# Seven block products in place of eight for q, k and r of a gated linear attention layer, in two phases with DRAM between them

## The chip, the cores and the metric

The kernel runs on one core of a Trainium2 chip, as one program with one launch. The metric is the device time of one execution in microseconds (us), from the first to the last instruction with what lies around them. The engines are TensorE (PE, matrix products into PSUM banks), VectorE (DVE), ScalarE (ACT), GpSimd (POOL) and SyncE (SP, which here issues nearly all DMA transfers). Each engine takes its own instructions strictly in the order in which the program has them, and waits on semaphores for what others make.

## The reference, cut to what matters

Two layers over a sequence of 1024 tokens with 1024 features, in float32: layer 0 has a mixer of a convolution module and an mLSTM, layer 1 has gated linear attention (GLA), and each layer ends in a SwiGLU FFN. The change touches layer 1's mixer:

```
def gla_mixer(h, w_in, gate_w2, gate_b, head_g, w_out):
    z = h @ w_in
    q, k, v, r, gl = jnp.split(z, [...], -1)
    log_alpha = log_sigmoid(gl @ gate_w2 + gate_b) / GLA_TAU
    o = gla_chunkwise(heads(q), heads(k), heads(v), heads(log_alpha))
    o = head_rmsnorm(o, head_g) * silu(r)
    return o @ w_out
```

There are 4 heads, each with 128 columns of q and of k and 256 of v and of r. h is the RMS-normed input of the layer. The result is added to the layer's input.

## The kernel before, in words

Activations are kept transposed: 8 tiles (k = 0 to 7) of 128 features by 512 tokens, for each of two halves of the tokens. A float32 product is made of three matmuls of a reduced type (`mm3`): every operand is cut into a high part (hH, wH; an ACT copy) and a low part (hL, wL; a DVE subtraction), `split` for activations and `weights` for a weight unit of 128 x 1024, which it loads (tile raw, 512 KB) and cuts (L163 on ACT, L164 on DVE). The matmuls of `mm3` are lines L170 (low weight), L171 (low activation) and L172 (both high). wH and wL have three buffers each, raw has two.

A projection `proj` of 128 columns for one half of the tokens is 8 k's times three matmuls, 24 matmuls of 128x512 into one PSUM bank "mm". The second mixer (`mixer1` with levels off) goes through the list ORDER1: p = v, q and k of a head; r = its r; x = the head's attention (decays, scores, state updates; banks "sm"), o = its norm, the transposes and the product with silu(r), whose result is y, two tiles a head and half, in SBUF; k0 = the cuts of y that the output projection needs. Where a letter a or b follows, only the first or second half of the tokens is meant. q and k leave their banks by an ACT copy (L827). silu(r) is made from a Tanh on ACT (L838) and one DVE operation (L839). x of head 3's second half and o of heads 2 and 3 stand behind k0 and are mixed with the first half of the output projection (`out_proj`, its run for half 0).

The order of each engine's instructions is fixed when the program is built, by a scheduler with a model of durations; `tc.high_priority(offset=...)` puts an instruction ahead of its place, which is how loads and weight cuts come early. SP's queue is one list: a transfer that waits for a buffer holds up all behind it. In layer 0 and in both FFNs the kernel already uses block products with sums of blocks and with DRAM in between.

There is a second branch in the program, the mixer with levels, run when a comparison (`fits`) says that the decays are too strong for the plain form.

Of the kernel before, what the change touches and what calls it, by code (L numbers as in the profile page):

```python
# [67 lines left out]
BOUND = -320.0  # L68

# [6 lines left out]
def trunk_kernel(ctx, tc, xT, cols, gate_b0, ev_vo0, ev_u, ev_cw, ev_out, od_v0, od_u, od_out, gate_w2, fin_row,  # L76
                 w13, w2, out, xsp, rowd, ud, zd, ad, x1, md):
# [627 lines left out]
    def mixer1(h, cut, then, levels):  # L705
        y = [[None, None] for _ in range(KT)]
        with tc.tile_pool(name="m1", bufs=1, reuse_waits="tile") as mp:
            unit = iter(range(30))
            masks = []
            if levels:  # L710
                for w in LEVELS:

                    nb = P // (2 * w)
                    m = mp.tile([P, nb, 2 * w], F32, tag="junk", name=f"mf{w}", bufs=1)
                    POOL.memset(m, 1.0)
                    for half, at in ((m[:, :, w:], 0), (m[:, :, :w], w)):

                        POOL.affine_select(out=half, in_=half, compare_op=ALU.is_ge, fill=0.0, base=-at,
                                           pattern=[[-2 * w, nb], [0, w]], channel_multiplier=1)
                        POOL.affine_select(out=half, in_=half, compare_op=ALU.is_ge, fill=0.0, base=at + w - 1,  # L720
                                           pattern=[[2 * w, nb], [0, w]], channel_multiplier=-1)
                    mu = mp.tile([P, P], U8, tag=f"mk{w}", name=f"mk{w}")
                    DVE.tensor_copy(mu, m.rearrange("p b x -> p (b x)"))
                    masks.append(mu)
                m = mp.tile([P, P], F32, tag="junk", name="mft", bufs=1)
                POOL.memset(m, 1.0)
                POOL.affine_select(out=m, in_=m, compare_op=ALU.is_ge, fill=0.0, base=-1, pattern=[[1, P]], channel_multiplier=-1)
                above = mp.tile([P, P], U8, tag="above", name="above")
                DVE.tensor_copy(above, m)
            else:  # L730
                m = mp.tile([P, P], F32, tag="junk", name="mft", bufs=1)
                POOL.memset(m, 1.0)
                POOL.affine_select(out=m, in_=m, compare_op=ALU.is_ge, fill=0.0, base=0, pattern=[[1, P]], channel_multiplier=-1)
                causal = mp.tile([P, P], U8, tag="causal", name="causal")
                DVE.tensor_copy(causal, m)
                whole = [mp.tile([P, HALF], F32, tag=f"A{i}", name=f"A{i}") for i in range(AB)]
                for t in whole:
                    POOL.memset(t, 0.0)
                least = mp.tile([P, HEADS, 2, 4], F32, tag="least", name="least")
# [37 lines left out]
            def decays(glc):  # L777

                es = []
                for half in range(2):  # L780
# [3 lines left out]
                    glr = mp.tile([P, HALF], F32R, tag="qt", name="glr", bufs=1 if levels else 2)  # L784
# [16 lines left out]
                for half in range(2):  # L801
                    for hd in range(HEADS):
# [6 lines left out]
                        if not levels:  # L809
                            DVE.tensor_copy(least[:, hd, half], lf.rearrange("p (c t) -> p c t", c=4)[:, :, P - 1])  # L810
                if not levels:
                    bounded()

            def bounded():

                m = mp.tile([P, 1], F32, tag="least1", name="least1")
                DVE.tensor_reduce(out=m, in_=least.rearrange("p a b c -> p (a b c)"), axis=mybir.AxisListType.X, op=ALU.min)
                b = bank("sm")
                PE.transpose(b[:1, :P], m, ident)
                n = mp.tile([1, 1], F32, tag="least2", name="least2")  # L820
                DVE.tensor_reduce(out=n, in_=b[:1, :P], axis=mybir.AxisListType.X, op=ALU.min)
                DVE.tensor_scalar(out=fits, in0=n, scalar1=BOUND, scalar2=None, op0=ALU.is_ge)

# [17 lines left out]
            def at_once(hd, half, q, k):  # L841

                A = whole[(2 * hd + half) % AB]
                pb = bank("sm")
                for c in range(4):
                    cs = slice(c * P, (c + 1) * P)
                    PE.matmul(pb[:, cs], k[:, cs], q[:, cs], start=True, stop=True)  # L847
                DVE.copy_predicated(A.rearrange("p (c t) -> p c t", c=4), causal.unsqueeze(1).to_broadcast([P, 4, P]),
                                    pb.rearrange("p (c t) -> p c t", c=4))
                return A  # L850

            def by_levels(bs, q, k):
# [43 lines left out]
                return A  # L896

            def head_mix(hd, half, q, k, v, st):
                bs = bsum[hd][half]
                b3 = bs.rearrange("p (c t) -> p c t", c=4)  # L900

                qt = mp.tile([P, HALF], F32, tag="qt", name=nm("qt"), bufs=1 if levels else 2)
                ACT.activation(qt, bs, AF.Exp, scale=1.0 / 16)
                ea = mp.tile([P, 4], F32, tag="ea", name=nm("ea"), bufs=2)
                ACT.activation(ea, b3[:, :, P - 1], AF.Exp, scale=1.0 / 16)
                DVE.tensor_tensor(out=qt, in0=qt, in1=q, op=ALU.mult)

                n = 4 - half
# [699 lines left out]
```

## Time and profile before

| What | Value |
|---|---|
| Time, median of 3 runs | 2133.81 us (2132.85 to 2134.03) |
| The profiled execution's own time, its span | 2133.76 us, 2132.0 us |
| Mean granted TensorE clock | 0.998 |
| Moved by DMA in the span | 279.04 MB, mean 131 GB/s |
| Second mixer's first matmul | at 1074.55 us |

The profile is of one execution. A line names the engine, the line of the program (L170), the tiles written and read without their numbers, the shape, and how long it was busy. PEld is the loading of weights into TensorE, which overlaps the matmuls. Matmuls are pipelined, so their busy times overlap; the distance of two starts is what one costs. "<- DVE wL L164" behind a wait names what ended it. A stretch of the span is given by its start and end in us; the share of busy time there belongs to that stretch alone. A letter q after an engine (SPq) is its queue of issues.

### The profile page before, as it was taken

The page shows a single profiled execution, that of the slowest core. Times are in us where ns is not written, and L with a number is a line of the kernel's source. Part 1 is how long each engine was busy: PE and PEld are TensorE (multiplying, and loading weights), DVE is VectorE, ACT ScalarE, POOL GpSimd, SP SyncE. Part 2 cuts the span into 40 slices and gives each one's busy share as a digit, 9 for nine tenths or more (in the row PEclk, how much of TensorE's full clock was granted, in tenths as well). Part 3 has the DMA queues.
Part 4 walks back from the last instruction along what each step waited for, and adds up shares of the span by engine and source line. Part 5 has one row for each costly group of instructions (what it writes and reads, how often), then busy time and mean ns, then how long its engine had stood idle before and what let it go on. Part 6 is the DMA issues. An engine that isn't in the chain of part 4 may idle for free.

```text
span 2132.0 us, 27718 instructions
## 1 busy us (share of the span) xinstructions
PE 2117.0 (99%) x10511; PEld 1795.9 (84%) x10511; DVE 1437.3 (67%) x2190; ACT 835.6 (39%) x1368; POOL 2.9 (0%) x15
## 2 busy tenths in 40 slices
PE   9999999999999999999999999999999999999998
PEld 8889988888888888888888989888888888888887
DVE  7555788777776666877875323367877666677686
ACT  6302327553222222444664434344522222235453
POOL 0000000000000000000000000000000000000000
PEclk9999999999999999999999999999999999999999
DMA  4233453654443334734421111154544333374344
GB/s 160 90 115 116 146 139 109 212 175 172 162 144 109 109 108 160 250 115 149 129 73 40 40 50 30 44 194 168 201 146 166 119 104 109 102 273 142 96 124 145
DMA packets 138222, 279.04 MB, mean 131 GB/s; under 512 B 22304, under 2 KB 35488, under 8 KB 138080
## 3 DMA queue, kind: packets, MB, share of 16 engines
q1 hardware_dynamic: 137808, 276.92, 39.6%
q8 instruction: 85, 1.39, 0.3%
q14 instruction: 57, 0.47, 0.1%
q10 hardware_dynamic: 272, 0.26, 0.0%
HBM read 210.51 MB, written 66.62 MB: 130 GB/s over the span
## 4 chain that ended last, share of the span: by engine, by line
PE 97%; DVE 1%; ACT 1%; DMA 1%; issue 0%; SPq 0%; DVEq 0%; ACTq 0%
PE mm L170 21%; PE mm L171 21%; PE mm L172 21%; PE sm L172 10%; PE sm L170 10%; PE sm L171 10%; PE sm L407 2%; PE sm L937 1%; PE sm L936 1%; PE sm L939 1%; DMA wb<-rowd 0%; PE sm L847 0%; PE sm L966 0%; PE sm L620 0%; PE sm L587 0%; PE sm L622 0%
## 5 line engine op out<-in xcount | busy, mean ns | idle before, releaser
L171 PE MATMUL mm<-hL,wH 128*128 128x512 f32 x1420 | 554.5, 391 | 0.2 <-DVE hL L335 0.2
L172 PE MATMUL mm<-hH,wH 128*128 128x512 f32 x1420 | 553.7, 390 | 0.0
L170 PE MATMUL mm<-hH,wL 128*128 128x512 f32 x1420 | 518.0, 391 | 2.1 <-DVE wL L164 1.2
L170 PEld LDWEIGHTS mm<-hH,wL 128*128 128x128 f32 x1420 | 266.5, 188 | 58.8 <-ACT hH L334 1.8
L171 PEld LDWEIGHTS mm<-hL,wH 128*128 128x128 f32 x1420 | 266.7, 188 | 55.9 <-DVE hL L335 1.0
L172 PEld LDWEIGHTS mm<-hH,wH 128*128 128x128 f32 x1420 | 266.7, 188 | 55.5 <-issue 0.2
L171 PE MATMUL sm<-hL,wH 128*128 128x512 f32 x616 | 240.1, 390 | 0.0
L172 PE MATMUL sm<-hH,wH 128*128 128x512 f32 x616 | 239.7, 389 | 0.0
L170 PE MATMUL sm<-hH,wL 128*128 128x512 f32 x616 | 209.0, 390 | 0.0
L143 ACT ACTIVATE wH<-S 128x1024 fp32r<-128x1024 f32 x88 | 93.3, 1060 | 214.1 <-PE sm L172 214.1
L143 ACT ACTIVATE wH<-q 128x512 fp32r<-128x512 f32 x143 | 90.4, 632 | 177.8 <-PE mm L172 100.6
L164 DVE TENSOR_TENSOR wL<-raw,wH 128x1024 fp32r<-128x1024 f32 (+2 forms) x77 | 94.2, 1223 | 82.6 <-ACT wH L163 82.4
L143 DVE TENSOR_TENSOR wL<-q,wH 128x512 fp32r<-128x512 f32 x143 | 98.6, 690 | 73.3 <-ACT wH L143 72.8
L170 PE MATMUL mm<-wH,hL 128*128 128x256 f32 (+2 forms) x512 | 146.4, 289 | 0.6 <-DVE xy L1320 0.6
L171 PE MATMUL mm<-wL,hH 128*128 128x256 f32 (+2 forms) x512 | 146.6, 287 | 0.0
L172 PE MATMUL mm<-wH,hH 128*128 128x256 f32 (+2 forms) x512 | 146.4, 287 | 0.0
L163 ACT ACTIVATE wH<-raw 128x1024 fp32r<-128x1024 f32 (+2 forms) x77 | 81.6, 1060 | 147.1 <-PE mm L172 115.2
L171 PEld LDWEIGHTS sm<-hL,wH 128*128 128x128 f32 x616 | 115.6, 188 | 24.7 <-issue 0.7
L170 PEld LDWEIGHTS sm<-hH,wL 128*128 128x128 f32 x616 | 115.6, 188 | 24.4 <-PE mm L172 0.5
L172 PEld LDWEIGHTS sm<-hH,wH 128*128 128x128 f32 x616 | 115.6, 188 | 24.3 <-issue 0.2
L143 DVE TENSOR_TENSOR wL<-S,wH 128x1024 fp32r<-128x1024 f32 x88 | 107.5, 1221 | 23.9 <-ACT wH L143 23.9
L1124 DVE TENSOR_TENSOR c<-sm,c 128x512 f32<-128x512 f32 x110 | 75.6, 687 | 70.5 <-PE sm L172 70.4
(324 smaller groups left out, 3434.6 us busy)
## 6 DMA issues: line engine op xcount, KB each, us to landing
raw<-in_w SPq DMA_DIRECT2D x108, 512.0 KB
mdT<-c SPq DMA_DIRECT2D x88, 256.0 KB
m<-mdT SPq DMA_DIRECT2D x88, 256.0 KB
mdB<-c SPq DMA_DIRECT2D x66, 256.0 KB
q<-in_w SPq DMA_DIRECT2D x60, 256.0 KB
m<-mdB SPq DMA_DIRECT2D x55, 256.0 KB
raw<-in_od_u SPq DMA_DIRECT2D x22, 512.0 KB
raw<-in_ev_u SPq DMA_DIRECT2D x20, 512.0 KB
```

Source lines behind the costliest of these rows:

```text
L143: ins = ACT.activation(dst[0], src, AF.Copy), lo.tensor_tensor(out=dst[1], in0=src, in1=dst[0], op=ALU.subtract)
L163: first = ACT.activation(hi, raw, AF.Copy)
L164: cuts = lo.tensor_tensor(out=low, in0=raw, in1=hi, op=ALU.subtract)
L170: return (PE.matmul(o, lt[1], rt[0], start=start and not on, stop=False, skip_group_check=on), PE.matmul(o, lt[0], rt[1], start=False, sto ...
L171: PE.matmul(o, lt[0], rt[1], start=False, stop=False, skip_group_check=on),
L172: PE.matmul(o, lt[0], rt[0], start=False, stop=stop, skip_group_check=on))
L407: PE.matmul(o, w[:, m * P:(m + 1) * P], raw[:, e, m:m + NT], start=m == 0, stop=m == SH)
L936: PE.matmul(db[:, cc, :], kw[:, cs], v[:, c, :], start=True, stop=True)
L937: PE.matmul(ob[:, cc, :], A[:, cs], v[:, c, :], start=True, stop=st is None)
L939: PE.matmul(ob[:, cc, :], qt[:, cs], st, start=False, stop=True)
L1124: DVE.tensor_tensor(out=out, in0=a, in1=b, op=ALU.add)
```

## The change

q and k of a head (or its two r tiles) are taken together as a product of 2 by 2 blocks: the weights are split by output column (two of 128) and by input feature (k = 0 to 3 and 4 to 7), the activations by input feature and by half of the tokens. The four results are c11, c12 (first column block, halves 0 and 1), c21 and c22. Eight block products of 12 matmuls become seven, with sums of weight blocks (tile S and in place in raw), sums of activation blocks (T1 to T4) and sums of results.

Phase one (list FIRST) makes the first column block's two products for half 0, A11 B11 and then A12 B21 in the same bank, and copies both states of the bank to DRAM (cd). It also makes v for all heads (those of heads 2 and 3 go to DRAM, vd) and the decays (to DRAM, bd). `transforms` makes T1 to T4 by 16 subtractions of unsplit activations; T1, T3 and T4 go to DRAM (td), T2 is cut at once; `operands` loads the three again and cuts them into the tiles that held h. Phase two (list REST) has for each pair the loads of both weight units, four sums of 512 columns, the cuts of two and a half units, the loads of the two phase-one results into the tiles of c12 and c11, and the products T2, T1, T3, T4 and B22, each a bank of its own but B22, which goes on top of T1's bank once that has been added; six sums read the banks. There are 8 pairs.

Silu is now one ACT function. y of heads 0 and 1 goes to DRAM (yd) and `get` loads it for the output projection: for half 0 into a tile of tag "q", for half 1 two at a time into a raw tile. The normed activations of the mixer's input are kept unsplit beside their parts. Before, the decays' Exp and Ln were made for both halves together, now for each half. The mixer with levels in the other branch stays as it was, and loses the code of the plain form.

```diff
+FIRST = 'q01 q23 v0 v1 v2 t v3 r01 r23'.split()
+REST = 'q0 q1 x0 r0 o0 q2 x1 f0 r1 o1 q3 x2 x3a r2 o2a r3 o3a k0 o2b x3b o3b'.split()
...
-    def mixer1(h, cut, then, levels):
+    def mixer1(h, cut, then):
...
+    def mixer1_at_once(h, b, cut, then):
...
+                        if hd < 2:
+                            ACT.activation(v[half][:, c, :], b[:, :256], AF.Copy)
+                        else:
+                            if c % 2 == 0:
+                                t = tmp()
+                            ACT.activation(t[:, c % 2 * 256:c % 2 * 256 + 256], b[:, :256], AF.Copy)
+                            if c % 2:
+                                SP.dma_start(vd[hd - 2, half][:, c // 2 * HALF:c // 2 * HALF + HALF], t)
...
+                        SP.dma_start(bd[hd, half], lf)
...
+            def first(kind, hds):
+                def aside(hd, i, b):
+                    with tc.high_priority(offset=WOFF):
+                        t = mp.tile([P, HALF], F32, tag="q", name=nm("c"), bufs=QB1)
+                        ACT.activation(t, b, AF.Copy)
+                        SP.dma_start(cd[spot(kind, hd), i], t)
+                ws, bs = [], []
+                for hd in hds:
+                    w, b = weights(od_u[at[kind, hd, 0]], 1024, DVE), bank("mm")
+                    for k in range(4):
+                        mm3(b, wcol(w, k, P), h[0][k], k == 0, k == 3)
+                    aside(hd, 0, b)
+                    ws.append(w)
+                    bs.append(b)
+                for hd, w, b in zip(hds, ws, bs):
+                    for k in range(4, KT):
+                        mm3(b, wcol(w, k, P), h[0][k], False, k == KT - 1, True)
+                    aside(hd, 1, b)
+            hv = {}
+            odd = [True]
+            def transforms():
+                for k in range(4):
+                    b11, b21, b12, b22 = b[0][k], b[0][k + 4], b[1][k], b[1][k + 4]
+                    for i, (o, x, z) in enumerate(((b11, b12, b11), (b12, b22, b12), (b22, b22, b11), (b21, b21, b22))):
+                        behind(DVE.tensor_tensor(out=o, in0=x, in1=z, op=ALU.subtract), made[1])
+                        if i != 2:
+                            SP.dma_start(td[min(i, 2), k], o)
+                    hv["T2", k] = tuple(hp.tile([P, HALF], F32R, tag=f"xy{k + 4 * i}_0", name=nm("T2")) for i in range(2))
+                    split(hv["T2", k], b22, DVE)
+                    hv["B22", k] = h[1][k + 4]
+            def operands():
+                for name, i, o, half in (("T1", 0, 0, 1), ("T3", 1, 0, 0), ("T4", 2, 4, 0)):
+                    for k in range(4):
+                        t = mp.tile([P, HALF], F32, tag="k", name=nm("t"), bufs=QB1)
+                        with tc.high_priority(offset=WOFF):
+                            SP.dma_start(t, td[i, k])
+                        hv[name, k] = hl(o + k, half)
+                        split(hv[name, k], t, DVE)
+            def cutw(x):
+                w = tuple(wp.tile([P, 1088], F32R, tag=t, name=nm(t))[:, :x.shape[1]] for t in ("wH", "wL"))
+                split(w, x, DVE)
+                return w
+            def pair(kind, hd, c11, c12, c21, c22):
+                with tc.high_priority(offset=WOFF):
+                    if odd[0]:
+                        r1, r2 = (mp.tile([P, 1024], F32, tag="raw", name=nm("raw"), bufs=2) for _ in range(2))
+                    else:
+                        r1, r2 = (wp.tile([P, 1088], F32, tag="raw", name=nm("raw"), bufs=2)[:, :1024] for _ in range(2))
+                    odd[0] = not odd[0]
+                    for i, t in ((1, r2), (0, r1)):
+                        SP.dma_start(t, od_u[at[kind, hd, i]])
+                    s = mp.tile([P, 1024], F32, tag="S", name=nm("S"), bufs=1)
+                    lo, hi = slice(0, HALF), slice(HALF, 1024)
+                    DVE.tensor_tensor(out=s[:, lo], in0=r2[:, lo], in1=r2[:, hi], op=ALU.add)
+                    DVE.tensor_tensor(out=s[:, hi], in0=s[:, lo], in1=r1[:, lo], op=ALU.subtract)
+                    w12 = cutw(s)
+                    DVE.tensor_tensor(out=r2[:, lo], in0=r1[:, lo], in1=r2[:, lo], op=ALU.subtract)
+                    w34 = cutw(r2)
+                    DVE.tensor_tensor(out=r1[:, hi], in0=r1[:, hi], in1=s[:, hi], op=ALU.subtract)
+                    w5 = cutw(r1[:, hi])
+                    SP.dma_start(c12, cd[spot(kind, hd), 0])
+                    SP.dma_start(c11, cd[spot(kind, hd), 1])
+                def prod(name, w, o, on=None):
+                    b = on if on is not None else bank("mm")
+                    for k in range(4):
+                        mm3(b, tuple(t[:, o + k * P:o + k * P + P] for t in w), hv[name, k], k == 0, k == 3, on is not None)
+                    return b
+                def add(o, b, x):
+                    DVE.tensor_tensor(out=o, in0=b, in1=x, op=ALU.add)
+                add(c12, prod("T2", w12, HALF), c12)
+                t = prod("T1", w12, 0)
+                add(c22, prod("T3", w34, 0), c12)
+                add(c21, prod("T4", w34, HALF), c22)
+                add(c22, t, c22)
+                add(c12, prod("B22", w5, 0, t), c12)
...
+                bs = mp.tile([P, HALF], F32, tag="bs", name=nm("bs"), bufs=4)
+                with tc.high_priority(offset=WOFF):
+                    SP.dma_start(bs, bd[hd, half])
...
+                    t = y[2 * hd + i][half]
+                    DVE.scalar_tensor_tensor(out=t, in0=b, scalar=c1(C_HG1 + 2 * hd + i), in1=t, op0=ALU.mult, op1=ALU.mult)
+                    if hd < 2:
+                        SP.dma_start(yd[2 * hd + i, half], t)
+            def get(k, half, d, _=None):
+                t = y[k][half]
+                if k < 4:
+                    if half == 0:
+                        t = mp.tile([P, HALF], F32, tag="q", name=nm("y"), bufs=QB1)
+                    else:
+                        if k % 2 == 0:
+                            ld[:] = [mp.tile([P, 1024], F32, tag="raw", name=nm("y"), bufs=2)]
+                        t = ld[0][:, k % 2 * HALF:k % 2 * HALF + HALF]
+                    with tc.high_priority(offset=1000):
+                        SP.dma_start(t, yd[k, half])
+                split(d, t, DVE)
...
+                if what[0] == "q":
+                    q, k = ([mp.tile([P, HALF], F32, tag=t, name=nm("qk"), bufs=QB1) for _ in range(2)] for t in "qk")
+                    pair("q", hd, *q, *k)
+                    heads[hd] = q, k
+                elif what[0] == "r":
+                    for i in range(2):
+                        for half in range(2):
+                            y[2 * hd + i][half] = hp.tile([P, HALF], F32, tag=f"xy{4 * (hd % 2) + 2 * i + half}_1", name=nm("y"))
+                    pair("r", hd, *y[2 * hd], *y[2 * hd + 1])
+                    for i in range(2):
+                        for t in y[2 * hd + i]:
+                            ACT.activation(t, t, AF.Silu)
...
+            r = rstd_half(xs)
+            d, work = [], []
+            for k in range(KT):
+                a = DVE.scalar_tensor_tensor(out=xs[k], in0=xs[k], scalar=c1(g + k), in1=r, op0=ALU.mult, op1=ALU.mult)
+                d.append(hl(k, half))
+                work += [[a], [split(d[k], xs[k], DVE)]]
...
+    layer(1, lambda cut, then: mixer1_at_once(h1, b1, cut, then), od_out, x1, C_FFN + 8, finish)
```

Three places show what moves. The line numbers of `mm3` are L172 to L174 in the new program; the numbers behind a tile's name only tell one tile from another, and they differ between the two programs.

The first place is on TensorE, in phase two, where the product B22 of the first pair stands: bank mm_10857 holds T1 of the pair of head 0's q and k, mm_10966 is the T3 of head 1's pair. In the new order:

```order
L172 MATMUL mm_10966<-hH_1907_10782,wL_10929 128x512
L173 MATMUL mm_10966<-hL_1908_10783,wH_10928 128x512
L174 MATMUL mm_10966<-hH_1907_10782,wH_10928 128x512
L172 MATMUL mm_10966<-hH_1910_10788,wL_10929 128x512
L172 MATMUL mm_10857<-hH_1729_9316,wL_10838 128x512
L173 MATMUL mm_10857<-hL_1730_9317,wH_10837 128x512
```

The twelve matmuls of B22 stand behind the T2, the T1 and ten matmuls of the T3 of the next pair; the two last matmuls of that T3 follow them.

The second place is SP's queue ahead of the first output projection: y tiles from yd, raw is a weight unit of the output projection, xy a tile of the layer's input. In the new order, where before there were only the raw and xy rows of these:

```order
L162 DMA raw_12277<-in_od_out 128x1024
L1247 DMA y_12117<-yd 128x512
L162 DMA raw_12311<-in_od_out 128x1024
L1247 DMA y_12123<-yd 128x512
L1247 DMA y_12129<-yd 128x512
L162 DMA raw_12345<-in_od_out 128x1024
L1247 DMA y_12135<-yd 128x512
L162 DMA raw_12379<-in_od_out 128x1024
L272 DMA xy_2355_12647<-x 128x512
```

The loads of y stand between the weight units, and the four tiles y follow one another through one buffer.

The third place is the start of that projection on TensorE: banks mm_11991 (before) and mm_12251, mm_12285, mm_12319 (now), with hH and hL the parts of y. Before:

```order
L170 MATMUL mm_11991<-hH_2118_11867,wL_11986 128x512
L171 MATMUL mm_11991<-hL_2119_11868,wH_11985 128x512
L172 MATMUL mm_11991<-hH_2118_11867,wH_11985 128x512
L170 MATMUL mm_11991<-hH_2120_11871,wL_11986 128x512
L171 MATMUL mm_11991<-hL_2121_11872,wH_11985 128x512
L172 MATMUL mm_11991<-hH_2120_11871,wH_11985 128x512
L170 MATMUL mm_11991<-hH_2122_11875,wL_11986 128x512
```

and now:

```order
L172 MATMUL mm_12251<-hH_2226_12127,wL_12246 128x512
L173 MATMUL mm_12251<-hL_2227_12128,wH_12245 128x512
L174 MATMUL mm_12251<-hH_2226_12127,wH_12245 128x512
L172 MATMUL mm_12285<-hH_2226_12127,wL_12280 128x512
L173 MATMUL mm_12285<-hL_2227_12128,wH_12279 128x512
L1203 MATMUL sm_11852<-v_11824,kw_11843 128x256
L174 MATMUL mm_12285<-hH_2226_12127,wH_12279 128x512
L172 MATMUL mm_12319<-hH_2220_12115,wL_12314 128x512
L173 MATMUL mm_12319<-hL_2221_12116,wH_12313 128x512
L172 MATMUL mm_12251<-hH_2229_12133,wL_12246 128x512
L172 MATMUL mm_12285<-hH_2229_12133,wL_12280 128x512
```

Before, the first bank takes tile after tile of y without a break; now three banks take each tile as it comes, with a state update (L1203) of head 3 between them.

On ACT the cuts of the same four tiles stood in one row (hH from xy, with two more behind):

```order
L143 ACTIVATE hH_2118_11867<-xy_1811_9880 128x512
L143 ACTIVATE hH_2120_11871<-xy_1820_9944 128x512
L143 ACTIVATE hH_2122_11875<-xy_1971_10944 128x512
L143 ACTIVATE hH_2124_11879<-xy_1980_11008 128x512
L143 ACTIVATE hH_2126_11883<-xy_2082_11612 128x512
L143 ACTIVATE hH_2128_11887<-xy_2091_11676 128x512
```

and now they stand among table loads, squares and Silus:

```order
L145 ACTIVATE hH_2220_12115<-y_12117 128x512
L1218 ACTIVATE junk_11764,ss_9357<-og_11732 128x256
L1224 ACT_TABLE_LOAD
L1224 ACTIVATE ss_9357<-ss_9357,epsc 128x4
L145 ACTIVATE hH_2223_12121<-y_12123 128x512
L165 ACTIVATE wH_12279<-raw_12277 128x1024
L1283 ACT_TABLE_LOAD
L1283 ACTIVATE y_12002<-y_12002 128x512
L1214 ACTIVATE og_11792<-sm_11794 128x512
L1283 ACTIVATE y_12003<-y_12003 128x512
L1218 ACTIVATE junk_11806,ss_9357<-og_11792 128x256
L145 ACTIVATE hH_2226_12127<-y_12129 128x512
```

What follows each cut on ACT now waits for the next load of y or for TensorE.

More of the change, by code (lines that the diff above doesn't have):

```diff
@@ L709, in mixer1 @@
             masks = []
[L710 to L725, printed above, removed]
-                POOL.memset(m, 1.0)
[L727 to L739, printed above, removed]
@@ new lines, in mixer1 @@
+            for w in LEVELS:
+                nb = P // (2 * w)
+                m = mp.tile([P, nb, 2 * w], F32, tag="junk", name=f"mf{w}", bufs=1)
+                POOL.memset(m, 1.0)
+                for half, at in ((m[:, :, w:], 0), (m[:, :, :w], w)):
+                    POOL.affine_select(out=half, in_=half, compare_op=ALU.is_ge, fill=0.0, base=-at,
+                                       pattern=[[-2 * w, nb], [0, w]], channel_multiplier=1)
+                    POOL.affine_select(out=half, in_=half, compare_op=ALU.is_ge, fill=0.0, base=at + w - 1,
+                                       pattern=[[2 * w, nb], [0, w]], channel_multiplier=-1)
+                mu = mp.tile([P, P], U8, tag=f"mk{w}", name=f"mk{w}")
+                DVE.tensor_copy(mu, m.rearrange("p b x -> p (b x)"))
+                masks.append(mu)
@@ L741, in mixer1 @@
+            m = mp.tile([P, P], F32, tag="junk", name="mft", bufs=1)
+            POOL.memset(m, 1.0)
+            POOL.affine_select(out=m, in_=m, compare_op=ALU.is_ge, fill=0.0, base=-1, pattern=[[1, P]], channel_multiplier=-1)
+            above = mp.tile([P, P], U8, tag="above", name="above")
+            DVE.tensor_copy(above, m)
             raw = tmp()
@@ L839, in head_r, with head_mix @@
                         DVE.scalar_tensor_tensor(out=t, in0=e, scalar=1.0, in1=b, op0=ALU.add, op1=ALU.mult)
[L841 to L852, printed above, removed]
+            def head_mix(hd, half, q, k, v, st):
+                bs = bsum[hd][half]
+                b3 = bs.rearrange("p (c t) -> p c t", c=4)
+                qt = mp.tile([P, HALF], F32, tag="qt", name=nm("qt"), bufs=1)
+                ACT.activation(qt, bs, AF.Exp, scale=1.0 / 16)
+                ea = mp.tile([P, 4], F32, tag="ea", name=nm("ea"), bufs=2)
+                ACT.activation(ea, b3[:, :, P - 1], AF.Exp, scale=1.0 / 16)
+                DVE.tensor_tensor(out=qt, in0=qt, in1=q, op=ALU.mult)
+                n = 4 - half
+                kt = tmp()[:, :n * P]
+                kt3 = kt.rearrange("p (c t) -> p c t", c=n)
+                DVE.tensor_tensor(out=kt3, in0=b3[:, :n, P - 1:P].to_broadcast([P, n, P]), in1=b3[:, :n], op=ALU.subtract)
+                ACT.activation(kt, kt, AF.Exp, scale=1.0 / 16)
+                DVE.tensor_tensor(out=kt, in0=kt, in1=k[:, :n * P], op=ALU.mult)
+                kb = bank("sm")[:, :n * P]
+                for c in range(n):
+                    PE.transpose(kb[:, c * P:(c + 1) * P], kt[:, c * P:(c + 1) * P], ident)
+                kw = mp.tile([P, HALF], F32, tag="kw", name=nm("kw"), bufs=1)[:, :n * P]
+                ACT.activation(kw, kb, AF.Copy)
                 A = mp.tile([P, HALF], F32, tag="A", name=nm("A"), bufs=AB)
@@ L1479, in trunk_kernel @@
             h.append(norm_half(xs, C_MIX + 8, half)[0])
-        layer(1, lambda cut, then: mixer1(h, cut, then, True), od_out, x1, C_FFN + 8, finish)
+        layer(1, lambda cut, then: mixer1(h, cut, then), od_out, x1, C_FFN + 8, finish)
 def _layout(i):
```

254 lines of the change are left out of this document (204 added, 50 removed).

## The prediction

> **What bounds the kernel now.** I read the page first (busy shares, then the chain that ended last), then what TensorE (PE) waits for, then the stretch of the second mixer. Page, part 1 and the first row of part 4:
>
> ```profile
> PE 2117.0 (99%) x10511; PEld 1795.9 (84%) x10511; DVE 1437.3 (67%) x2190; ACT 835.6 (39%) x1368; POOL 2.9 (0%) x15
> ...
> PE 97%; DVE 1%; ACT 1%; DMA 1%; issue 0%; SPq 0%; DVEq 0%; ACTq 0%
> ```
>
> PE is busy for 2117.0 of 2132.0 us and 97% of the chain runs through it. What PE waits for in the whole span (in total, times, longest):
>
> ```profile
> PE sm L105 <- DVE t L102: 1.5, 1, 1.5
> PE mm L170 <- DVE wL L164: 1.2, 2, 0.6
> PE mm L170 <- ACT hH L334: 0.9, 1, 0.9
> PE mm L170 <- DVE xy L1320: 0.6, 1, 0.6
> PE sm L622 <- DVE st L628: 0.4, 2, 0.2
> PE mm L171 <- DVE hL L335: 0.2, 1, 0.2
> ```
>
> These add to 4.8 us, and only the 0.6 us on L1320 is at the second mixer's door. So matmuls taken away are time taken away, as long as the others keep up. How far they are from the edge is read by stretches (us; busy PE, PEld, DVE, ACT, POOL; granted clock; DMA share; GB/s): the second mixer up to the first half of its output projection, then a piece of layer 0's FFN and one of layer 1's:
>
> ```profile
> 1074.00:1440.00 366.00, 365.45 (x2060) 322.42 (x2061) 163.24 (x266) 162.31 (x291) 0.00 (x0) 1.00 0.21 69
> ...
> 852.80:906.10 53.30, 53.30 (x237) 44.14 (x236) 45.60 (x74) 23.05 (x41) 0.00 (x0) 1.00 0.73 250
> ...
> 1865.50:1918.80 53.30, 53.30 (x237) 44.14 (x236) 37.91 (x55) 16.85 (x25) 0.00 (x0) 1.00 0.77 274
> ```
>
> In the mixer PE leaves out 0.55 of 366 us, VectorE (DVE) works 45%, ScalarE (ACT) 44%, and DMA moves 69 GB/s. In the FFN pieces PE loses nothing while DVE is at 86% and DMA at 250 to 274 GB/s. That is the yardstick for a mixer that is to be fuller.
>
> **What the change removes from PE.** The price of a 128x512 matmul is its pitch in a steady run, not its busy time:
>
> ```profile
> 1241.10 0.39 PE L172 MATMUL mm<-hH,wH 128*128 128x512 f32 x1
> ...
> 1250.16 0.39 PE L170 MATMUL mm<-hH,wL 128*128 128x512 f32 x1
> ```
>
> Forty matmuls lie between these starts: 9.06 / 40 = 0.2265 us. A pair (q and k of a head, or the two r columns) had four halves of 24 matmuls, 96. Now it has 24 in phase one and five products of 12 in phase two, 84. Eight pairs lose 96 matmuls: 96 x 0.2265 = 21.7 us. The head's matmuls and transposes stay in number.
>
> **What it adds beside PE.** Prices from the groups of the stretch from 1070 to 1440, by form (count, busy, mean ns):
>
> ```profile
> L164 DVE TENSOR_TENSOR wL<-raw,wH 128x1024 fp32r<-128x1024 f32 x31 | 37.8, 1221 | 63.0 <-ACT wH L163 62.9
> L163 ACT ACTIVATE wH<-raw 128x1024 fp32r<-128x1024 f32 x31 | 32.8, 1059 | 74.2 <-PE mm L172 73.7 <-ACT kw L925 0.5
> ...
> L839 DVE SCALAR_TENSOR_TENSOR xy<-t,mm 128x512 f32<-128x512 f32 x16 | 10.9, 681 | 10.7 <-ACT t L838 10.7
> L957 ACT ACT_TABLE_LOAD x8 | 10.3, 1283 | 0.1
> L143 DVE TENSOR_TENSOR hL<-xy,hH 128x512 fp32r<-128x512 f32 x16 | 10.1, 684 | 0.0
> ...
> L143 ACT ACTIVATE hH<-xy 128x512 fp32r<-128x512 f32 x16 | 9.5, 627 | 4.6 <-DVE xy L968 4.4
> ...
> L1320 DVE TENSOR_TENSOR xy<-xy,mm 128x512 f32<-128x512 f32 x4 | 2.5, 680 | 0.0
> ```
>
> - DVE: q, k and r had 16 weight units of 1024 columns to cut in two. Now they have 8 in phase one and 2.5 for each of 8 pairs in phase two, 28: 12 more x 1.22 = 14.6. Weight sums 32 x 0.68 = 21.9 and sums on product banks 48 x 0.68 = 32.6 (as L1320, which also reads a bank), 16 differences of the activations 10.9, 16 more cuts 10.9, less 16 of L839 (-10.9). Together +80 us: 163 + 80 = 243 of 366 - 21.7 = 344 us, 71%.
> - ACT: 12 units x 1.06 + 16 cuts x 0.63 = 22.8; copies aside take the place of the copies of q and k, and Silu that of Tanh, at equal number. With up to 10 more table loads of 1.28 it is about +29 to +36, 56 to 58% of the stretch.
> - DMA: 16 weight units of 0.52 MB become 24 (phase two reads phase one's 8 again), 4.2 MB more; phase one's results take 32 transfers of 0.26 MB, transforms 24, decays 16, y 16, v as much as 16: 104 x 0.26 = 27 MB. The stretch had 69 GB/s x 366 us = 25 MB, now 56 MB in 344 us: 165 GB/s.
>
> 71% and 165 GB/s are below the 86% and 250 GB/s that the FFN hides, so as an average this costs PE nothing. Without that cover 80 us of DVE would be far more than the gain, so what counts is each place where PE's next operand is made just in time.
>
> **Where PE may wait in the products.** One chain makes a pair's first operand: load, two sums, a cut on ACT and one on DVE. The nearest rows for a load are these two issues and their first users:
>
> ```profile
> 1.27 0.41 SPq L315 DMA_DIRECT2D raw<-in_ev_u  x1
> ...
> 4.16 0.63 ACT L143 ACTIVATE wH<-raw 128x512 fp32r<-128x512 f32 x1 [1.75 <-DMA raw<-in_ev_u]
> ```
>
> ```profile
> 1071.82 0.33 SPq L160 DMA_DIRECT2D raw<-in_od_v  x1
> ...
> 1075.23 1.11 ACT L163 ACTIVATE wH<-raw 128x1088 fp32r<-128x1088 f32 x1 [0.16 <-DMA raw<-in_od_v]
> ```
>
> 256 KB took 2.9 us and 544 KB 3.4. So 3.4 + 2 x 0.68 + 1.06 + 1.22 = 7.0 us from issue to first product. A pair is 60 matmuls in phase two, 13.6 us, and its weight tiles are three of three buffers: a cut may start only when the tile's last reader is done. The order puts the product of one pair that reads the last tile (B22) some 34 matmuls behind that pair's T4, among the next pair's products, so that two sums on DVE (1.4 us) stand against 7.7 us of PE. The typical cover of a cut is two products, 24 x 0.2265 = 5.4 us, against 2.3. Tightest is the first r pair, whose T2 waits for a tile that q0's B22 read last: there the cover is about as long as the chain. I put 0 to 1 us there, 0 to 1 for the first product phase (its T4 operands come back from DRAM and are cut one by one) and 0 to 1.5 spread over the rest: 1 us in sum, bounds 0 and 3.5.
>
> **Where it will wait: the reload of y.** Before, the cuts of y for the output projection came straight from SBUF. Now y of heads 0 and 1 lies in DRAM. The four tiles of half 0 come back one behind the other through one buffer, each load waiting for the DVE cut of the one before: 2.9 + 0.63 + 0.69 = 4.2 us a link, 16.9 us for four. The first load can go only when head 2 has read its q of half 0 for the last time. From there to the first use of the fourth tile the order holds 58 matmuls of 512 columns and 27 of 256 and 128. These are priced by the nearest form:
>
> ```profile
> 1074.75 0.29 PE L171 MATMUL mm<-wL,hH 128*128 128x272 f32 x1
> ...
> 1074.88 0.29 PE L172 MATMUL mm<-wH,hH 128*128 128x272 f32 x1
> ```
>
> 0.13 us each, at most. That is 13.1 + 3.5 = 16.6 us of PE work against 16.9 - 0.7 = 16.2 to the fourth tile's high part: just on time with nothing in the way, 2 late if each load takes 3.4. But ACT and DVE serve their queues in order. Between these cuts ACT now has four or five table loads (1.28 each), Silus that wait for the last r products and squares of head 2; DVE has weight cuts of 1.22 and sums of 0.68 that wait for PE in turn. One table load or unit cut in each of four links is +5 us. The projection's banks are therefore interleaved tile by tile, and every late tile stops three banks and the heads' scores queued behind them on PE. Bounds: nothing, if the scheduler's spacing holds, and 9 (2 + 5 + 2, the last for one unit cut and one sum that head 3's scores and state updates wait for behind the same queue). I take 5: the chain is on time only with empty queues, and they are full.
>
> Sum, against the profiled execution (2133.76 us, its span 2132.0 and 1.76 around it): 2133.76 - 21.7 + 1 + 5 = 2118 us. The median of the runs shown, 2133.81, is the same to 0.05. Without the terms of waiting it is 2112; with both upper bounds 2112 + 3.5 + 9 = 2124.5.
>
> **Rivals.**
> 1. Everything is hidden, the tail too. For it: PE waits 4.8 us in 2132 at loads like these. Against: no tile before came back through one buffer in four dependent links. 2110 to 2114 us.
> 2. The product stage runs just in time at every pair. DVE's share there is above the mean of 71%: 60 matmuls' 13.6 us hold 4 sums, 2.5 cuts and 6 bank sums, 9.9 us, beside the head's own work. If a DVE instruction that waits for a bank holds up the next pair's cut once per pair by a unit cut and a sum, 1.9 us, it is 8 x 1.9 = 15 less what the 1 us already has: 2118 + 14 = 2132, half of it 2125. For it: the weight cuts and the bank sums share one queue in order. Against: the FFN rows at 86%.
> 3. Slower: the SP queue holds up the weight loads. SP issues in order, and each pair's loads stand behind reloads of phase one's results, which wait for tiles that a head still reads. SP does wait long:
>
> ```profile
> SPq L160 <- DVE wL L164: 329.9, 55, 34.7
> ...
> SPq L1070 <- DVE S L1077: 204.2, 38, 9.1
> ```
>
> If a waiting reload keeps the next pair's weights from being issued until that pair is due, PE stands for the 7.0 us chain at each of 8 pairs: +56, 2168. It decides the sign from (21.7 + 4.3) / 8 = 3.3 us per pair on: over 2138. Against: two sets of raw buffers let loads go a pair ahead, and the FFN's SP waits of up to 9.1 us cost PE nothing.
> 4. One long gap in the tail instead of small ones: a whole link of 4.2 us late at one tile, with PE then slow for as long again. No stretch shown has a granted clock under 1.00, and the longest wait is 1.5 us, so no row prices the second part; between nothing and 4.2 more it is 2118 to 2122. [...]
> 5. The change doesn't do what it says: the second program branch with levels runs, or the matmuls don't fall. The instruction order has 97 rows fewer on PE (14,764 before, 14,667 now), so this has little chance.
>
> **Numbers.** Forecast (2114 to 2124, likeliest 2118) 0.50; everything hidden 0.20; just in time 0.16, a bit more than half of it still clearly faster; slower by the queue 0.07; one long gap 0.05; not as said 0.02. With 0.2% (4.3 us, about what a measurement of this kernel can tell from no change) that makes faster 0.50 + 0.20 + 0.09 + 0.05 = 0.84, same 0.07 + 0.02 = 0.09, slower 0.07. The range for 8 in 10 is 2111 to 2127: it holds the forecast, nearly all of the hidden case and the lower half of the just-in-time one.
>
> **What would show it.** Right: 96 matmuls fewer of 128x512, the mixer's stretch shorter by about 15 us, DVE near 70% and 155 to 175 GB/s in it, and waits of PE on hH and hL of y at the first output projection, made up of small ones, 3 to 8 us together. Wrong: waits of PE on wL or wH of 1 us and more in each pair (rival 2), the same behind DMA raw (rival 3), a clock under 1.00 behind the tail (rival 4), or none at all (rival 1).

## The result

The changed kernel takes 2120.97 us (median of 4 runs, 2120.06 to 2121.11) against 2133.92 before (4 runs, 2132.85 to 2134.96). The ratio is 0.9938, 95% interval 0.9921 to 0.9956: 13 us, 0.6% faster. The profiled execution took 2121.00 with a span of 2119.3.

The page of the changed kernel, part 1 and the first row of part 4:

```profile
PE 2099.7 (99%) x10415; PEld 1781.1 (84%) x10415; DVE 1504.2 (71%) x2294; ACT 863.4 (41%) x1413; POOL 2.9 (0%) x15
...
PE 96%; DVE 1%; ACT 1%; DMA 1%; issue 0%; SPq 0%; DVEq 0%; ACTq 0%
```

There are 96 matmul records fewer (10,511 before), DVE has 67 us more of busy time in the span and ACT 28. DMA moved 310.52 MB in place of 279.04. What TensorE waits for, the same view as before (total, times, longest):

```profile
PE mm L173 <- DVE wL L166: 3.1, 1, 3.1
PE mm L172 <- ACT hH L336: 1.6, 2, 1.2
PE sm L107 <- DVE t L104: 1.5, 1, 1.5
PE mm L172 <- DVE wL L166: 0.6, 1, 0.6
PE mm L172 <- DVE y L1154: 0.6, 1, 0.6
PE sm L624 <- DVE st L630: 0.4, 2, 0.2
PE mm L172 <- DVE xy L1614: 0.3, 1, 0.3
PE mm L173 <- DVE hL L337: 0.3, 1, 0.3
PE sm L1043 <- DVE glr L1037: 0.2, 1, 0.2
PE mm L172 <- ACT hH L145: 0.2, 1, 0.2
```

Of the waits that the prediction looked for, those on hH and hL of y at the output projection come to 0.2 us (the last row), and this one is for a y of head 2 that VectorE has just made, not for a reloaded tile. The row on L1154 is a sum of the last r pair and costs 0.6; further down it is followed back to the reload. No wait on wL stands in a pair. The largest row is new and one piece, 3.1 us. The stretch of the mixer up to the last head's transposes, after and then before (us; PE, PEld, DVE, ACT, POOL; clock; DMA share; GB/s):

```profile
1074.00:1417.14 343.14, 338.62 (x1919) 297.92 (x1918) 224.58 (x363) 186.40 (x331) 0.00 (x0) 1.00 0.46 154
```

```profile
1074.00:1431.24 357.24, 356.69 (x2018) 314.99 (x2018) 157.51 (x258) 158.70 (x286) 0.00 (x0) 1.00 0.20 63
```

DVE went from 44 to 65%, ACT from 44 to 54%, DMA from 63 to 154 GB/s. The stretch is 14.1 us shorter. TensorE lacks 4.5 us in it, before 0.55.

**The new gap.** It lies in phase one, where head 2's v is made. TensorE stops inside a projection of 128x256 matmuls, and this is what VectorE (DVE) does there (timeline of the changed kernel with ACT and TensorE beside it: start, busy us; L1053 and L1056 make the decays of the second half of the tokens, L166 cuts a weight unit):

```profile
1151.83 1.37 DVE L1056 TENSOR_TENSOR_SCAN bs<-one,bs 128x128 f32<-128x128 f32 x4
...
1152.02 1.05 ACT L165 ACTIVATE wH<-raw 128x1024 fp32r<-128x1024 f32 x1
...
1153.12 0.67 DVE L1053 TENSOR_TENSOR bs<-bs,e 128x512 f32<-128x512 f32 x1
...
1153.70 2.63 DVE L1056 TENSOR_TENSOR_SCAN bs<-one,bs 128x128 f32<-128x128 f32 x8
...
1154.16 0.28 PE L172 MATMUL mm<-wH,hL 128*128 128x256 f32 x1
1156.24 1.21 DVE L166 TENSOR_TENSOR wL<-raw,wH 128x1024 fp32r<-128x1024 f32 x1
...
1157.50 0.39 PE L173 MATMUL mm<-wL,hH 128*128 128x256 f32 x1 [3.06 <-DVE wL L166]
```

The second weight unit's high part stood ready at 1153.07 on ACT, 3.2 us ahead of the cut of its low part. That cut stands in VectorE's queue behind twelve scans, whose results go to DRAM for phase two; eight of them, and one L1053, ran while it could have. VectorE doesn't rest in this part: it is busy for 24.97 of the 25 us from 1141 to 1166. And behind the gap the granted clock is not 1.00 (same columns as above):

```profile
1157.50:1159.00 1.50, 1.50 (x12) 1.50 (x13) 1.50 (x3) 0.00 (x0) 0.00 (x0) 0.94 0.64 195
1159.00:1160.00 1.00, 1.00 (x6) 1.00 (x6) 1.00 (x5) 0.38 (x1) 0.00 (x0) 0.50 0.97 289
1160.00:1161.00 1.00, 1.00 (x7) 1.00 (x6) 1.00 (x4) 0.00 (x0) 0.00 (x0) 0.50 0.92 332
1161.00:1162.00 1.00, 1.00 (x7) 1.00 (x7) 1.00 (x2) 0.38 (x1) 0.00 (x0) 0.50 1.05 393
1162.00:1163.00 1.00, 1.00 (x9) 1.00 (x9) 1.00 (x4) 0.00 (x0) 0.00 (x0) 0.89 0.98 361
```

For 3.4 us (1158.81 to 1162.22) TensorE runs at a granted clock of 0.50: its matmuls start 0.21 us apart where they start 0.12 apart before and behind. So the theory to be tested was: one late weight cut costs 3.1 us of standing and some 1.6 of slow running, and the tail, where the prediction had put its 5 us, costs little. The rivals: the low clock has another cause; the cut is late for its load or buffer; the pairs lose time too, spread thin.

### The profile page after: what moved, and what is told of

Same layout as the page of the kernel before. It is cut to its first block, busy times and chain, and to the rows that moved or that the text cites. A ratio compares the mean times of both kernels' runs of the same rounds, so it can differ in the third digit from the quotient of the medians.

```text
span 2119.3 us, 27932 instructions
## 1 busy us (share of the span) xinstructions
PE 2099.7 (99%) x10415; PEld 1781.1 (84%) x10415; DVE 1504.2 (71%) x2294; ACT 863.4 (41%) x1413; POOL 2.9 (0%) x15
## 2 busy tenths in 40 slices
DMA packets 153776, 310.52 MB, mean 147 GB/s; under 512 B 24032, under 2 KB 37216, under 8 KB 153632
## 4 chain that ended last, share of the span: by engine, by line
PE 96%; DVE 1%; ACT 1%; DMA 1%; issue 0%; SPq 0%; DVEq 0%; ACTq 0%
PE mm L172 20%; PE mm L173 20%; PE mm L174 20%; PE sm L174 10%; PE sm L172 10%; PE sm L173 10%; PE sm L409 2%; PE sm L1204 1%; PE sm L1206 0%; PE sm L1203 0%; PE sm L622 0%; PE sm L1231 0%; PE sm L1192 0%; PE sm L589 0%; PE sm L624 0%; DVE bs L1056 0%
## 5 line engine op out<-in xcount | busy, mean ns | idle before, releaser
L173 PE MATMUL mm<-hL,wH 128*128 128x512 f32 x1356 | 531.0, 392 | 0.3 <-DVE hL L337 0.3
L174 PE MATMUL mm<-hH,wH 128*128 128x512 f32 x1356 | 529.1, 391 | 0.0
L172 PE MATMUL mm<-hH,wL 128*128 128x512 f32 x1356 | 495.0, 393 | 3.4 <-ACT hH L336 1.6
L172 PEld LDWEIGHTS mm<-hH,wL 128*128 128x128 f32 x1356 | 254.7, 188 | 58.1 <-ACT hH L336 2.5
L173 PEld LDWEIGHTS mm<-hL,wH 128*128 128x128 f32 x1356 | 255.2, 188 | 53.6 <-DVE hL L145 0.7
L174 PEld LDWEIGHTS mm<-hH,wH 128*128 128x128 f32 x1356 | 255.0, 188 | 53.2 <-issue 0.2
L174 PE MATMUL sm<-hH,wH 128*128 128x512 f32 x616 | 239.9, 389 | 0.0
L172 PE MATMUL sm<-hH,wL 128*128 128x512 f32 x616 | 209.1, 391 | 0.0
L145 ACT ACTIVATE wH<-S 128x1024 fp32r<-128x1024 f32 x96 | 101.7, 1060 | 222.8 <-PE sm L174 213.5
L174 PE MATMUL mm<-wH,hH 128*128 128x256 f32 (+2 forms) x512 | 146.4, 287 | 0.0
L172 PE MATMUL mm<-wH,hL 128*128 128x256 f32 (+2 forms) x512 | 145.1, 287 | 0.2
L145 DVE TENSOR_TENSOR wL<-S,wH 128x1024 fp32r<-128x1024 f32 x96 | 117.3, 1222 | 29.3 <-ACT wH L145 29.3
L172 PEld LDWEIGHTS sm<-hH,wL 128*128 128x128 f32 x616 | 115.7, 188 | 24.4 <-PE mm L174 0.5
L174 PEld LDWEIGHTS sm<-hH,wH 128*128 128x128 f32 x616 | 115.7, 188 | 24.2 <-issue 0.2
L145 ACT ACTIVATE wH<-raw 128x1024 fp32r<-128x1024 f32 (+1 forms) x86 | 85.8, 999 | 122.3 <-PE sm L174 67.9
L166 DVE TENSOR_TENSOR wL<-raw,wH 128x1024 fp32r<-128x1024 f32 (+2 forms) x69 | 84.4, 1224 | 44.0 <-ACT wH L165 39.0
```

Of the source, the lines that this page charges most:

```text
L145: ins = ACT.activation(dst[0], src, AF.Copy), lo.tensor_tensor(out=dst[1], in0=src, in1=dst[0], op=ALU.subtract)
L166: cuts = lo.tensor_tensor(out=low, in0=raw, in1=hi, op=ALU.subtract)
L172: return (PE.matmul(o, lt[1], rt[0], start=start and not on, stop=False, skip_group_check=on), PE.matmul(o, lt[0], rt[1], start=False, sto ...
L173: PE.matmul(o, lt[0], rt[1], start=False, stop=False, skip_group_check=on),
L174: PE.matmul(o, lt[0], rt[0], start=False, stop=stop, skip_group_check=on))
```

## The experiments

**The gap closed.** The scans of the second half are put behind the cut; every instruction and every value stays. `scans` collects the scans (16 for each half), `made[1]` is the last cut, and `behind` orders two instructions of one engine:

```diff
                     wa, wb = (weights(od_u[at["v", hd] + i], 1024, DVE) for i in range(2))
+                    if hd == 2:
+                        for scan in scans[16:]:
+                            behind(scan, made[1])
```

> The scans of the second half's decays are put behind the cut of the last weight unit of head 2's v on VectorE; nothing else changes and the result is the same. The changed kernel lost 3.06 us of TensorE there (wait on wL, ended by L166) and then ran at a granted clock of 0.50 for 4 us (estimated loss 1.5 to 2.0 us). Theory (the queue of VectorE makes the gap, and the gap lowers the clock): the wait goes, the clock stays at 1.00, and the time falls by 4.6 to 5.1 us, from 2121.0 to about 2116. Rival 1 (the gap only, the low clock has another cause): the time falls by 3.1 us, to 2118, and a stretch at 0.50 remains. Rival 2 (the unit's load or its buffer is late as well): the wait shrinks by less than half and stays above 1.5 us.

Measured: 2115.33 us median (2114.92 to 2118.54), ratio to before 0.9913 (0.9897 to 0.9930). The wait is gone and the clock is 1.00 in each microsecond from 1158 to 1166. Single executions scatter by 1 to 4 us (a product of layer 0 waited 2.1 us in this profile, 1.2 in the other), so the traces are compared on a stretch that holds the same 531 matmul records in every kernel: from the second group of the decays' matmuls to the first product of phase two. Changed kernel, then the gap closed:

```profile
1139.61 1.20 PE L1043 MATMUL sm<-glr,gw 128*128 128x512 f32 x4 [0.21 <-DVE glr L1037]
...
1218.00 0.39 PE L172 MATMUL mm<-T,wL 128*128 128x512 f32 x1
```

```profile
1141.39 1.20 PE L1048 MATMUL sm<-glr,gw 128*128 128x512 f32 x4 [0.20 <-DVE glr L1042]
...
1215.12 0.39 PE L172 MATMUL mm<-T,wL 128*128 128x512 f32 x1
```

78.39 us become 73.73: 4.66 us, the gap's 3.06 and 1.60 more. The queue of VectorE made the gap, and what lay behind the gap went with it.

**The gap shorter and longer.** Only the last two groups of scans are put behind the cut (one group of 1.3 us fewer ahead of it than in the changed kernel), or all four ahead of it:

The shorter:

```diff
+                    if hd == 2:
+                        for scan in scans[24:]:
+                            behind(scan, made[1])
```

and the longer:

```diff
+                    if hd == 2:
+                        behind(made[1], scans[-1])
```

> One group of four scans (1.37 us) is put behind the same cut, so the gap should be 1.7 us in place of 3.06. If any wait of this size lowers the clock in proportion to its length: 2121.0 - 1.4 - 0.7 = 2118.9, with some 2 us at 0.50. If the clock falls only from some length on, and 1.7 us is below it: 2121.0 - 1.4 - 1.7 = 2117.9 and no stretch under 1.00. If the low clock has another cause: 2119.6 with the same 4 us at 0.50.

> All four groups of scans stand before the same cut, so the gap should be 3.06 + 1.3 + 0.1 = 4.5 us. If the time at half clock is one stretch of fixed length: 2121.0 + 1.4 = 2122.4, with about 4 us at 0.50 as now. If it grows with the gap by the same measure: 2123.1 and about 6 us at 0.50. If the gap is not made by this queue: 2121.0.

Measured: 2118.9 us (2117.1 to 2118.97) and 2122.35 (2121.46 to 2123.86). Waits of the shorter and the longer, and the longer one's clock:

```profile
PE mm L173 <- DVE wL L166: 1.8, 1, 1.8
```

```profile
PE mm L173 <- DVE wL L166: 4.4, 1, 4.4
...
1156.00:1158.00 2.00, 0.00 (x0) 0.00 (x0) 2.00 (x5) 0.00 (x0) 0.00 (x0) 0.81 0.74 219
1158.00:1160.00 2.00, 1.91 (x9) 1.91 (x10) 2.00 (x4) 0.21 (x1) 0.00 (x0) 0.50 0.79 252
1160.00:1162.00 2.00, 2.00 (x11) 2.00 (x11) 2.00 (x7) 0.38 (x1) 0.00 (x0) 0.50 1.12 295
1162.00:1164.00 2.00, 2.00 (x11) 2.00 (x11) 2.00 (x4) 0.38 (x1) 0.00 (x0) 0.50 0.86 323
1164.00:1166.00 2.00, 2.00 (x19) 2.00 (x18) 2.00 (x5) 0.38 (x1) 0.00 (x0) 0.98 1.03 396
```

After the gap of 1.79 us the clock was 1.00 throughout; after 4.39 us it was 0.50 for some 6 us of work, and had begun to fall inside the gap. The same 531 matmuls take 75.64 and 80.85 us:

| Gap, us | 531 matmuls, us | over no gap | beyond the gap itself |
|---|---|---|---|
| 0 | 73.73 | 0 | 0 |
| 1.79 | 75.64 | 1.91 | 0.12 |
| 3.06 | 78.39 | 4.66 | 1.60 |
| 4.39 | 80.85 | 7.12 | 2.73 |

So the loss isn't in proportion: there is next to none after 1.79 us. The whole times alone would have said otherwise. The shorter gap came to 2118.9, which is what a loss in proportion called for, where a threshold called for 2117.9; but the clock in its profile stays at 1.00, and that profile has 0.4 us of a wait on wL in a pair and 0.4 more on another cut, which the first profile of the changed kernel doesn't have. The longer came to a median of 2122.35, which is what a slow stretch of fixed length called for (2122.4); its profiled execution took 2123.01, and there the slow stretch is twice as long as in the changed kernel. So the claims here rest on the stretch of 531 matmuls and on the clock, in one profile each of the shorter and the longer gap.

**96 matmuls put back.** T2 is made twice in its bank in every pair (the sums then hold it twice):

```diff
-                add(c12, prod("T2", w12, HALF), c12)
+                add(c12, prod("T2", w12, HALF, prod("T2", w12, HALF)), c12)
```

> The product T2 of each pair is made twice in the same bank, 12 matmuls more a pair, 96 in all, which is the number that the change took away (the sums then hold T2 twice, so the result is another). Theory (the pairs are bound by TensorE alone): 96 x 0.2265 = 21.7 us more, 2142.7. Rival (in the pairs TensorE is paced by VectorE or by loads): part of the 96 falls into waits, and the time grows by less than 18 us.

Measured: 2143.46 us (2143.15 to 2143.90), 22.5 over the changed kernel. All 96 show, so the pairs are bound by TensorE and the price per matmul holds. With as many matmuls as before, the new arrangement is 9.6 us slower than the kernel before (2133.84 in that comparison; ratio 1.0046, 1.0029 to 1.0063): that is its own cost.

**More work for VectorE.** In seven pairs the weight sums are twice taken to the maximum with themselves, ahead of their cut:

```diff
+                    if (kind, hd) != ("q", 0):
+                        for _ in range(2):
+                            DVE.tensor_tensor(out=s, in0=s, in1=s, op=ALU.max)
                     w12 = cutw(s)
```

> Seven of the eight pairs (not the first) get two more VectorE operations of 128x1024 on the weight sums, ahead of their cut (each the maximum of the tile with itself, so the values stay): 14 x 1.22 = 17 us more on VectorE, and 2.4 us more in the chain from the weights to each pair's first product. Theory (the products' operands are made far enough ahead, VectorE has room): 0 to 2 us more than the changed kernel's 2121.0. Rival (just in time, the second rival of the prediction): a wait on wL or on hL in each of these pairs, together 10 to 17 us, so 2131 to 2138.

Measured: 2122.94 us (2122.12 to 2124.03), 2.0 more. Most of it is one row of its waits:

```profile
PE sm L1234 <- DVE og L1230: 1.3, 1, 1.3
```

17 us more of VectorE cost 2 in all, and no wait on a pair's weights came with it. From 1230 to 1368 VectorE was busy 111.40 of 138 us there (81%; 102.39 in the changed kernel). The pairs aren't just in time.

**The reload of y twice.**

```diff
-                        SP.dma_start(t, yd[k, half])
+                        for _ in range(2 - half):
+                            SP.dma_start(t, yd[k, half])
```

> Each of the four tiles y of half 0 is loaded twice from DRAM, the second load behind the first: 2.9 us more in each of four links, 11.6 us in all, everything else as in the changed kernel. In its trace the last of the four loads lands about 1.6 us ahead of its cut on ScalarE and the cut ends 0.2 to 0.8 us ahead of TensorE's use. Theory (the chain of reloads runs with little to spare, as the prediction had it): 6 to 10 us of waits of TensorE on hH or hL of y at the first output projection, 2127 to 2131. Rival (the reload is far ahead of its use, and the 5 us predicted were never near): less than 2 us.

Measured: 2120.99 us (2118.89 to 2122.53), no change; TensorE's wait on hH of y stays at 0.2, and is for head 2's y as before. The expectation of 6 to 10 us failed. But the experiment is not clean: with more transfers the scheduler also placed TensorE's work anew, and moved head 3's scores and some state updates ahead of the late tiles. It shows that there was work to put there, not how much reserve the first order had.

**The weights of the pairs twice.** Each of the 16 loads of phase two is made twice:

```diff
-                        SP.dma_start(t, od_u[at[kind, hd, i]])
+                        for _ in range(2):
+                            SP.dma_start(t, od_u[at[kind, hd, i]])
```

> Phase two loads both weight units of each pair twice, the second load behind the first: 16 loads of 0.52 MB more, 3.4 us more on each unit and more issues in SP's queue. Theory (loads are issued a pair ahead): 0 to 2 us more than 2121.0. Rival (SP's queue holds up the weight loads, the third rival of the prediction): waits behind the loads in each of 8 pairs, 13 us and more together, 2134 or later.

Measured: 2129.48 us (10 runs, 2127.57 to 2132.11), 8.5 more and between the two expectations. Its waits in the mixer:

```profile
PE mm L173 <- DVE wL L166: 3.0, 1, 3.0
PE mm L172 <- DVE wL L145: 2.2, 1, 2.2
...
PE sm L1207 <- DVE st L1212: 1.5, 2, 1.1
PE sm L1204 <- DVE st L1212: 1.2, 2, 1.0
PE sm L1204 <- ACT kw L1187: 0.8, 1, 0.8
```

One pair's first product is late by 2.2 us (head 1's q and k), and heads' small steps by 3.5; the rest of the 8.5 us isn't assigned. What holds up that pair is not a load of weights, as rival 3 has it. The cut of its weight sums stands in VectorE's queue behind a sum of head 0's pair, and this one waits for the reload of a phase-one result (cd):

```profile
1230.44 0.69 DVE L1155 TENSOR_TENSOR qk<-mm,qk 128x512 f32<-128x512 f32 x1 [1.75 <-DMA qk<-cd]
...
1231.71 1.22 DVE L145 TENSOR_TENSOR wL<-S,wH 128x1024 fp32r<-128x1024 f32 x1
```

That is the queue of rival 2, in one pair and not in eight, with a load behind it. The same sum waits 0.51 us for its reload in the changed kernel, where TensorE doesn't wait for the cut, 1.04 with the shorter gap (TensorE waits 0.4) and 1.08 with the reloads of y (1.0): head 1's q and k is where the new arrangement runs closest.

**The two side by side.** The changed kernel and the closed gap again, on one chip.

> The changed kernel as it is, beside the next one on one chip. The wait of 3.0 us on wL stands in every execution, the low clock behind it in most but not all (it was missing in one of the six profiles that had a gap of 3.0 us), so single times should scatter over about 1.6 us: 2119 to 2121.5, median near 2121.

> The same with the second half's scans behind the weight cut (no gap, clock at 1.00). By the stretch from the second group of decay matmuls to the first product of phase two (531 matmuls, 78.39 against 73.73 us) it should be 4.7 us faster than the changed kernel in the executions where that one's clock falls, 3.1 where it doesn't: median 2116 to 2116.5. If it is not at least 3 us faster, the gap's time comes back elsewhere.

Measured (five profiles with such a gap, not six, had come before): 2121.03 us (2119.89 to 2121.46; ratio 0.9942, 0.9929 to 0.9956) and 2116.67 (2115.52 to 2117.35; ratio 0.9921, 0.9908 to 0.9935). The second is a little above the 2116 to 2116.5 expected. There are 4.4 us between the medians, 4.68 by the 531 matmuls (78.41 and 73.73). This reordering is faster than both kernels, 0.8% under the one before.

## Why the prediction came out as it did

The time, 2120.97 for 2118, and the sign were right; where the difference to the full gain goes was not. Of 21.7 us of matmuls 12.7 came out in the spans of the two profiles; 9.0 were lost where 6 had been put.

- **The matmuls taken away, 21.7 us: right.** 96 records fewer, and putting 96 back cost 22.5.
- **Beside TensorE: right as an average.** +67 us of DVE in the stretch for +80. A pair has five sums that read a bank, not six as counted (40 of L1154 in the trace, not 48), which makes 5.4 us of the difference; the rest is that operations in a row overlap (1.90 us for three of L1103, 0.63 each in place of 0.68); ACT +27.7 for +29 to +36; 154 GB/s for 165. None of it costs TensorE as an average.
- **"1 us in sum" for the products: right for the pairs, and the place was left out that mattered.** No wait on a pair's weights stands in the trace, and 17 us more of VectorE there cost 2. But the working looked for just-in-time places in phase two only. Phase one packs the decays, the first pair's weight sums and v's cuts into one stretch in which VectorE never rests, and there the cut of head 2's v came 3.06 us late. Of rival 4 ("one long gap") the slow running behind a gap came true, at another place than the tail: the granted clock was 0.50 for 3.41 us behind the gap of 3.06, which cost 4.66.
- **"I take 5" for the tail: mis-sized.** The reload's first issue came right behind head 2's last read of q (L1206, to 1355.6), as worked out. The four loads, and the use of the fourth tile on TensorE:

```profile
1355.66 0.32 SPq L1247 DMA_DIRECT2D y<-yd  x1
...
1362.70 4.63 SPq L1247 DMA_DIRECT2D y<-yd  x2
...
1371.83 0.32 SPq L1247 DMA_DIRECT2D y<-yd  x1
...
1376.27 0.61 ACT L145 ACTIVATE hH<-y 128x512 fp32r<-128x512 f32 x1
...
1377.07 0.40 PE L172 MATMUL mm<-hH,wL 128*128 128x512 f32 x1
```

From the first issue to the cut of the fourth tile's high part the chain took 21.2 us, not the bare 16.2: the 5 us of holdups in ACT's and DVE's queues are there. But TensorE took 21.4 us over the same stretch, 0.6 of it the wait on L1154, so the cover was 20.8 us and not 16.6. The step that failed is the price of the small matmuls, "0.13 us each, at most", taken from a reduced-type product of 272 columns. The heads' matmuls are plain float32, and each stands in the trace as two records (56 of L936 before, for the program's 28 state updates). Rows of the kernel before would have shown it:

```profile
1157.60 1.03 PE L937 MATMUL sm<-v,A 128*128 128x256 f32 x4
1158.47 0.59 PE L936 MATMUL sm<-v,kw 128*128 128x256 f32 x2
1158.90 0.59 PE L937 MATMUL sm<-v,A 128*128 128x256 f32 x2
```

One matmul, two records, takes 0.43 us (1158.47 to 1158.90), three times the price taken. So the small matmuls from 1355.66 to 1377.07, 24 records of 256 columns and 21 of 128 (0.10 us each, as 1355.79 to 1356.61 for eight of L1192), come to about 7.3 us where 3.5 had been put. The cover was about as long as the chain, and TensorE waited for none of the four reloaded tiles themselves. The 0.6 us on L1154 come from them by another way:

```profile
1365.63 0.63 ACT L145 ACTIVATE hH<-y 128x512 fp32r<-128x512 f32 x1 [2.97 <-DMA y<-yd]
...
1366.29 0.69 DVE L145 TENSOR_TENSOR hL<-y,hH 128x512 fp32r<-128x512 f32 x1 [1.92 <-ACT hH L145]
1366.90 1.41 DVE L1154 TENSOR_TENSOR y<-mm,y 128x512 f32<-128x512 f32 x2
```

ACT waits for the second tile's load, VectorE for ACT, and the sums that TensorE needs stand behind that cut in VectorE's queue; TensorE goes on at 1368.36. Between 1362 and 1408 it lost some 2 us over its matmuls' steady pitches, 0.8 of it this wait and the one on head 2's y; what made the rest is not shown.

The rest of the 9.0, beyond 4.7 of the gap and about 2 of the tail: 0.5 was lost before the mixer began (the last matmul of layer 0 starts at 1074.11, before at 1073.60), 0.2 is a wait on glr, and some 2 us are not assigned. (The 0.35 us on L1614 at the mixer's door were 0.56 before, on L1320.) That the sum came within 3 us of the time is in part luck, errors of opposite sign: 3 us or more too many for the tail and 1 for the products, 5 too few for phase one and 2 for what is not assigned.

The rivals: everything hidden (2110 to 2114) isn't reached even with the gap closed, which gives 2115 to 2117. Just in time in every pair is refuted by the run with more VectorE work, a queue of SP that stalls every pair by the changed kernel's waits.

## What to carry to other kernels

Where work is moved to another phase, look at that phase's fullest stretch on each in-order engine, and at what TensorE needs from behind the slow operations there. A mean of 65% busy says nothing about 25 us without a pause. Price a small matmul by the starts of its own row and data type; a product of like width in another type was off by a factor of three here (0.13 us for 0.43). And a gap of TensorE cost half as much again as its length here (4.66 us for 3.06), where a shorter one cost its length alone (1.91 for 1.79): order what nobody waits for behind what TensorE does wait for.

## What the runs showed of the hardware

TensorE's granted clock fell to 0.50 around a single gap of 3.0 to 3.1 us in five of the six profiles that had one, and stayed at 1.00 in the sixth (the weights twice: 76.93 us for the 531 matmuls, where the others took 78.2 to 78.4). Where it fell, and for how long, follows to about 0.1 us from its means over stretches of 1 to 4 us:

| Profile | Gap, us | End of the gap | Clock 0.50 from, to | 531 matmuls, us |
|---|---|---|---|---|
| Gap shorter | 1.79 | 1156.32 | stayed at 1.00 | 75.64 |
| Weights twice | 3.05 | 1158.03 | stayed at 1.00 | 76.93 |
| Changed kernel | 3.06 | 1157.50 | 1158.8, 1162.2 | 78.39 |
| T2 twice | 3.06 | 1157.84 | 1159.0, 1162.4 | 78.42 |
| Reload of y twice | 3.04 | 1157.17 | 1156.8, 1160.2 | 78.22 |
| More VectorE work | 3.04 | 1157.44 | 1157.1, 1160.6 | 78.29 |
| Changed kernel again | 3.05 | 1156.26 | 1156.6, 1160.0 | 78.41 |
| Gap longer | 4.39 | 1158.09 | 1157.2, 1164.1 | 80.85 |

The five low stretches that go with a gap of 3.0 to 3.1 us lasted about 3.4 us each, and the one with the longer gap 6.8. The clock fell anywhere from 0.4 us ahead of the end of such a gap to 1.3 us behind it. So the length of the gap alone doesn't settle it: a gap of 3.05 us left the clock at 1.00 in one profile and went with 0.50 in another. What settles it is not shown. All eight are single profiles of one place of one program.
